# Moving context's residual and norm, half of a modulation, and the deal of fill work in a two-layer hybrid mixer

## The chip, the cores and the metric

The kernel runs on one core of a Trainium2 chip. The metric is the device time of one execution in microseconds, as the median of several runs. A core has five engines that this text names as the profile does: PE (TensorE, matmuls; PEld is its weight load), DVE (VectorE), ACT (ScalarE), POOL (GpSimd) and SP, which here only issues DMAs. Each engine takes its instructions in program order, and an instruction that waits holds up those behind it.

## The reference

Two layers act on 256 latent tokens x and 256 context tokens, 1024 wide, in fp32. Each layer normalises and modulates its input, makes one wide projection from it, feeds three token mixers (rwkv-7, neighbourhood attention, differential attention), merges the three by gates, and projects back. Cut to what matters:

```python
for l in range(2):
    mod_x, mod_c = silu(c) @ w_mod[l] + b_mod[l], silu(c_ctx) @ w_mod[l] + b_mod[l]   # shift, scale, gate
    hx  = rmsnorm(x)  * (1 + sc_x) + sh_x
    hcn = rmsnorm(hc) * (1 + sc_c) + sh_c
    z = h @ w_in[l]                            # inputs of the three mixers, their gates, the merge gates
    o = rwkv7(z), neighbourhood(z), differential(z)
    yb = stack([o_b * silu(g_b)]) @ w_branch[l]              # three branches
    y = sum(sigmoid(mg) * yb) @ w_out[l]
    x  = x  + gt_x * rmsnorm(y_x)
    hc = hc + gt_c * rmsnorm(y_c)              # not in the last layer
return x
```

## The kernel before

Every matmul is done in three passes over fp32r halves (`mm3`): each weight chunk is loaded by SP into a `wr` tile (256 KB, 128x512), ACT copies its high part to `wh`, DVE subtracts to get the low part `wl`, and PE does high by high, high by low and low by high. All operations go through helpers, so the profile's lines are the helpers': L164 ACT, L167 DMA, L179 reduction, L185 two tensors, L189 tensor and scalar, L192 scalar and two tensors, L195 matmul, L199 transpose. A framework places tiles in pools, sets the semaphores and orders each engine's instructions; `keep_in_program_order` pins some of them to the order of the code. General tiles come from one slab of 52 slots, named `k`; PSUM tiles are named `z`, `a`, `b` and `y`.

A layer runs as follows. `rwkv` and `attn` are generators of main work, with waits on chains of small operations, and `weave` deals fill work beside them: after each step of the main generator the table `yl` (L142, one dict for each layer) says how many microseconds of fill are owed, and fill is taken until the debt is paid. The fill is the wide projection's chunks for later mixers (`z_pair`, matmuls of 128x256 or 128x512), gates, merge gates, and the merges of the first two branches. In `yl`, `step` is what is paid after an rwkv step, `qq` and `inv` after parts of the triangular inverse, `diff` after a unit of differential attention and `nd` after the norm of a pair of its heads. A pair of numbers is indexed by segment, head pair or half of the queries; in layer 1 only the first number of `diff` is ever used.

Then `merge(l, 2)` does the third branch: eight output blocks `dt`, each 12 matmuls of 128x512, with wb loads on SP, merge gates `md` loaded on POOL's queue, and POOL adding the blocks. `merged` splits the sums. `outproj` multiplies by wo in 16 chunks and calls `ahead(i)` after each chunk's split, which loads rows of x and context (`rows_load`), loads the next layer's modulation weights wm (`mod_load`, 32 chunks of 256 KB into slab slots), and takes steps of `mod_rows`. A step of `mod_rows` multiplies one wm chunk (`y<-k,cs`); after each eight of them it adds a bias row on DVE (`k<-y,k`, L185), transposes it on PE (`z<-cst,k`) and stores scale and shift for a quarter of the features (`mA`, `mB`). `derived` makes a dozen small per-layer constants on DVE, in a fixed order.

`outproj` ends with `done(t)` for the four token tiles: tiles 0 and 1 are x, and get `residual` (square sum, rsqrt by small DVE operations, two `k<-y,s,k`) and `norm_row` (squares on ACT, rsqrt, scaling) at once; tiles 2 and 3 are context and are put off to `late`. `stream_in` transposes normed rows to features and modulates them. `start_next` starts the next layer with x alone: a `z_pair` for rwkv, the late context rows (`ctx[0]`), the two chunks of the first gate (`gates`: `z_pair`, a tanh on ACT, a multiply `gs<-gs,z` on DVE, a store), and then context's `stream_in` (`ctx[1]`).

Of the kernel before, what the change touches and what calls it, by code (L numbers as in the profile page):

```python
# [134 lines left out]
class K:  # L135
    def __init__(self, tc, io, out):
        self.tc, self.nc, self.io, self.out = tc, tc.nc, io, out
        self.n = 0
        self.have = {}
        self.in_order = False  # L140

        self.yl = [dict(inv=(57, 42.0), qq=(6, 12.07), step=(6, 6), na=(2.5, 1.19), diff=(2.3, 2.9), q=(1.0, 1.0), nd=(2.75, 5), A=(0, 0), B=(0, 4), G=(0.75, 0), C=(5.6, 7.2)),  # L142
                   dict(inv=(23, 51), qq=(3.0, 1.5), step=(6, 6), na=(1.0, 2.3), diff=(4.69, 8.12), q=(1.0, 1.0), nd=(0, 2), A=(0, 0), B=(4.5, 0), G=(0.75, 0), C=(4.0, 6.0))]


    def count(self):
# [335 lines left out]
    def start_next(self, l, P, nr, ctx):  # L482

        r = self.now(self.z_pair(l, 0, 0, nr))
        self.rwkv_rows(l, P, 0, 1, r, 0, nr, False)
        ctx[0]()
        self.now(self.gates(l, nr, 0))
        ctx[1]()
        self.rwkv_wa(l, P, self.now(self.z_pair(l, 6, 0, T)), 0, T)
        row = [self.rwkv_rows(l, P, 0, w, self.now(self.z_pair(l, c, 0, T)), 0, T, True) for w, c in ((0, 2), (2, 4))]  # L490
        self.have["rx", l, 0] = True
        self.have["rz", l, 0] = row[0], [None, None], row[1]
# [889 lines left out]
    def run(self):  # L1382
        tc, nc, io = self.tc, self.nc, self.io
        with ExitStack() as es:
            pool = lambda name, bufs, **kw: es.enter_context(tc.tile_pool(name=name, bufs=bufs, **kw))
            self.const = pool("const", 1)
            self.par = pool("par", 1)
            self.slab = pool("slab", NSLOT)
            self.wr, self.wh, self.wl = pool("wr", 6), pool("wh", 5), pool("wl", 4)
            self.k4 = pool("k4", 7)  # L1390
            self.smp = pool("smp", 8)
            self.pi = pool("pi", 1)
            self.inv = pool("inv", 1)
            self.st = pool("st", 1)
            self.gs, self.gl = pool("gs", 2), pool("gl", 2)
            self.psp = pool("psp", 2, space=PSUM)
            self.psb = {"z": 3, "y": 1}
            dr = pool("dr", 1, space=DRAM)
            dt_ = lambda n, shape: dr.tile(list(shape), F32, tag=n, name=n)
            pairs = lambda n, l, m: [dt_(f"{n}{l}_{i}", (128, 2, T)) for i in range(m)]  # L1400
            self.gd = [pairs("gd", l, 6) for l in range(L)]
            self.md = [pairs("md", l, 12) for l in range(L)]
            self.od = [pairs("od", l, 2) for l in range(L)]
            self.qd = [[pairs(f"qd{w}_", l, 2) for w in range(2)] for l in range(L)]
            self.kd = [[pairs(f"kd{w}_", l, 2) for w in range(2)] for l in range(L)]
            self.rd = [[dt_(f"rd{l}_{g}", (128, 2, 3, T)) for g in range(2)] for l in range(L)]
            self.vd = [[dt_(f"vd{l}_{w}", (128, 4, 512)) for w in range(2)] for l in range(L)]
            self.td = [dt_(f"td{l}", (4, 2, 256)) for l in range(L)]
            self.xd = dr.tile([NX, 1024], F32, tag="xd", name="xd")
            self.cvec()  # L1410
            xs = []
            for t in range(4):
                o = self.k4.tile([128, 2, 512], F32, tag="k4", name=f"x{t}")
                self.dma(self.nc.sync, o, io["xt"][128 * t:128 * t + 128].rearrange("p (a b) -> p a b", a=2))
                xs.append([o[:, 0, :], o[:, 1, :]])
            cst = self.const.tile([128, NCC], F32, tag="cst", name="cst")
            self.dma(nc.gpsimd, cst, io["cst"])
            for k, (a, b) in CCOL.items():
                setattr(self, k, cst[:, a:b])
            P = self.params(0)  # L1420
            ws = []
            self.start(0, P, xs, self.mod_rows(0, P, ws), ws)
            for l in range(L):
                last = l == L - 1
                nq = NX if last else T
                acc = [None] * 8
                PN = None if last else self.params(l + 1)

                def mods():
                    if l == 0:  # L1430
                        yield from self.mod_gate(l, P)
                    if not last:
                        yield from self.mod_gate(l + 1, PN)

                def zs():
                    if l == 0:
                        yield from self.gates(l, nq, 0)
                    if l == 0:
                        yield from self.gates(l, nq, 1)
                        yield from self.rwkv_z(l, P, 1, 0, T, T)  # L1440
                    else:
                        yield from self.rwkv_z(l, P, 1, 0, T, nq)
                        yield from self.gates(l, nq, 1)
                    yield from self.mgates(l, nq, 0)
                    yield from self.attn_z(l, 0, nq)
                    yield from self.attn_z(l, 1, nq)
                    yield from self.gates(l, nq, 2)
                    yield from self.mgates(l, nq, 1)
                    yield from self.mgates(l, nq, 2)

                fill = self.chain(self.both(mods(), zs()), self.merge(l, 0, acc, nq), self.merge(l, 1, acc, nq))
                self.weave(self.rwkv(l, P, last), fill, False)
                self.weave(self.attn(l, P, last), fill)
                self.now(self.merge(l, 2, acc, nq))
                s = self.merged(acc, nq)
                xsrc = io["xt"] if l == 0 else self.xd

                ws, xs, late = [], [], []
                if not last:
                    self.derived(l + 1, PN)  # L1460
                    self.h_new()
                    mod = self.mod_rows(l + 1, PN, ws)

                def ahead(i):
                    if i % 4 == 3 and i // 4 < (2 if last else 4):
                        self.rows_load(xsrc, i // 4, xs)
                    if not last:
                        self.mod_load(l + 1, ws, 2 * i - 4)
                        for _ in range(2 if i > 6 else 0):
                            next(mod)  # L1470

                def rows(t, y, ss):
                    self.residual(t, y, ss, xs[t], last)
                    if not last:
                        self.norm_row(xs[t])

                def done(t, y, ss):
                    if t < 2:
                        rows(t, y, ss)
                    else:  # L1480
                        late.append((t, y, ss))

                self.outproj(l, s, 1 if last else 2, ahead, done)
                if not last:
                    self.mod_load(l + 1, ws, 32)
                    self.now(mod)
                    self.stream_in(PN, xs[0:2], 0)
                    self.start_next(l + 1, PN, NX, (lambda: [rows(*a) for a in late],
                                                    lambda: self.stream_in(PN, xs[2:4], 1)))
                P = PN  # L1490
# [63 lines left out]
```

## Time and profile before

| what | value |
|---|---|
| runs | 1428.95, 1429.24, 1432.83 us, median 1429.24 |
| profiled execution | 1424.81 us, its span 1423.1 us |
| mean granted TensorE clock | 0.966 of full speed |
| PE busy | 1320.4 us (93%) |
| PEld busy | 1098.9 us (77%) |
| DVE busy | 995.7 us (70%) |
| ACT busy | 779.2 us (55%) |
| POOL busy | 233.6 us (16%) |
| moved by DMA | 212.42 MB, mean 149 GB/s |

Times in views are from the start of the span. Layer 0's third merge begins at 737 us, the output projection at 759, and layer 1's first projection matmul stands at 833.13. The idle time that a row of the timeline gives in brackets lies just ahead of that instruction, and the name behind the arrow is what ended it.

### The profile page before, as it was taken

Reading aid. Unit: us, or ns where it says so; the run is one execution under the profiler, and the core shown is the slowest. Engines: PE = TensorE matmul, PEld = TensorE weight load, DVE = VectorE, ACT = ScalarE, POOL = GpSimd, SP = SyncE. Lnnn points to the kernel's source line nnn. Section 1 sums busy time; section 2 is a strip of 40 time slices with the busy share of each in tenths; the row PEclk is TensorE's granted clock in tenths of the full one; section 3 lists DMA queues with packets and bytes.
Section 4 is the critical chain, followed back from the end, with each engine's and each line's share of the span. In section 5 each row is a group of like instructions: output and inputs, shape, how many; then the busy total and the mean of one; then the engine's idle time right before and its main releaser. Section 6 shows DMA issues by size and latency. Waiting matters only on the chain. (4 is left out here: it accounts for less than half of the span.)

```text
span 1423.1 us, 28637 instructions
## 1 busy us (share of the span) xinstructions
PE 1320.4 (93%) x10784; PEld 1098.9 (77%) x10784; DVE 995.7 (70%) x2117; ACT 779.2 (55%) x1734; POOL 233.6 (16%) x292
## 2 busy tenths in 40 slices
PE   6998999999999999998999889998999999999897
PEld 4866777889779876677778777888878789867687
DVE  4763469836898368778685386768848893679886
ACT  5462375336863446667433255866449634467653
POOL 0010011012110012224253000101111000122441
PEclk9999999999999999999999999999889999999899
DMA  9466642424324267432545844354513252685454
GB/s 356 129 196 200 208 130 82 128 68 157 119 80 121 77 185 222 155 105 93 178 145 168 324 127 119 113 177 126 170 56 105 68 148 69 182 272 154 141 166 154
DMA packets 112987, 212.42 MB, mean 149 GB/s; under 512 B 13088, under 2 KB 24880, under 8 KB 112848
## 3 DMA queue, kind: packets, MB, share of 16 engines
q1 hardware_dynamic: 102896, 178.33, 40.6%
q0 software_dynamic: 9952, 32.26, 7.0%
q8 instruction: 85, 1.39, 0.4%
q14 instruction: 54, 0.44, 0.1%
HBM read 176.70 MB, written 33.83 MB: 148 GB/s over the span
## 5 line engine op out<-in xcount | busy, mean ns | idle before, releaser
L195 PE MATMUL z<-k,wh 128*128 128x512 f32 (+1 forms) x2352 | 653.9, 361 | 8.8 <-ACT wh L164 4.2
L195 PEld LDWEIGHTS z<-k,wh 128*128 128x128 f32 x2352 | 417.8, 194 | 76.2 <-issue 9.1
L195 PE MATMUL z<-k,wl 128*128 128x512 f32 (+1 forms) x1176 | 421.7, 360 | 7.3 <-DVE wl L185 7.3
L164 ACT ACTIVATE wh<-wr 128x512 fp32r<-128x512 f32 x376 | 235.4, 630 | 317.8 <-PE z L195 212.7
L185 DVE TENSOR_TENSOR wl<-wr,wh 128x512 fp32r<-128x512 f32 x376 | 278.5, 747 | 157.7 <-PE z L195 59.9
L195 PEld LDWEIGHTS z<-k,wl 128*128 128x128 f32 x1176 | 227.1, 194 | 42.8 <-DVE wl L185 12.1
L195 PE MATMUL z<-wh,k 128*128 128x256 f32 x736 | 145.1, 291 | 2.6 <-ACT k L164 1.3
L195 PEld LDWEIGHTS z<-wh,k 128*128 128x128 f32 x736 | 119.6, 196 | 5.7 <-DVE k L192 2.1
L195 PE MATMUL z<-wl,k 128*128 128x256 f32 x368 | 106.7, 290 | 0.6 <-DVE wl L185 0.6
L185 POOL TENSOR_TENSOR k<-k,k 64x512 fp32r<-64x512 f32 (+3 forms) x64 | 78.0, 1222 | 154.9 <-ACT k L164 62.1
L164 ACT ACTIVATE gs<-z 128x512 f32<-128x512 f32 (+1 forms) x134 | 66.7, 500 | 53.5 <-PE z L195 44.1
L164 ACT ACTIVATE k<-k 64x256 fp32r<-64x256 f32 (+5 forms) x146 | 74.8, 537 | 32.0 <-POOL k L185 20.3
L185 DVE TENSOR_TENSOR k<-k,k 128x256 fp32r<-128x256 f32 (+5 forms) x134 | 76.0, 580 | 12.0 <-ACT k L164 9.3
L199 PE MATMUL b<-cst,k 128*128 128x128 f32 x368 | 65.1, 286 | 17.6 <-DVE k L189 5.6
L164 ACT ACTIVATE k<-a,s 128x512 f32<-128x512 f32 (+1 forms) x96 | 59.2, 617 | 33.1 <-DVE s L179 32.1
L195 PEld LDWEIGHTS z<-wl,k 128*128 128x128 f32 x368 | 72.2, 196 | 1.4 <-DVE wl L185 1.0
L199 PEld LDWEIGHTS b<-cst,k 128*128 128x128 f32 x368 | 42.9, 144 | 37.6 <-issue 15.0
L164 ACT ACTIVATE k<-b 128x256 f32<-128x256 f32 (+1 forms) x144 | 62.8, 465 | 16.5 <-PE b L199 15.8
L195 PE MATMUL a<-k,k 128*128 128x512 f32 (+1 forms) x192 | 61.1, 404 | 10.0 <-ACT k L164 6.1
L195 PE MATMUL a<-ar,bk 64*128 64x128 f32 (+1 forms) x512 | 51.1, 288 | 9.6 <-ACT Lab L164 8.8
L195 PEld LDWEIGHTS a<-ar,bk 64*128 64x128 f32 x512 | 43.5, 190 | 21.3 <-ACT Lab L164 15.7
L179 DVE TENSOR_REDUCE s<-a 128x1 f32<-128x512 f32 (+1 forms) x96 | 56.4, 588 | 1.2 <-PE a L195 1.0
(175 smaller groups left out, 1899.4 us busy)
## 6 DMA issues: line engine op xcount, KB each, us to landing
wr<-in_wi SPq DMA_DIRECT2D x296, 256.0 KB, 3.1
k<-in_wm SPq DMA_DIRECT2D x64, 256.0 KB, 5.4
wr<-in_wb SPq DMA_DIRECT2D x48, 256.0 KB, 2.6
md<-gs SPq DMA_DIRECT2D x36, 256.0 KB, 2.9
k<-md POOLq DMA_DIRECT2D x36, 256.0 KB, 4.5
wr<-in_wg SPq DMA_DIRECT2D x32, 256.0 KB, 3.4
wr<-in_wo SPq DMA_DIRECT2D x32, 256.0 KB, 4.0
gd<-gs SPq DMA_DIRECT2D x18, 256.0 KB, 3.2
```

The lines of the kernel that those rows point to most:

```text
L164: return self.nc.scalar.activation(out=out, in_=in_, func=func, **kw)
L179: return self.nc.vector.tensor_reduce(out=out, in_=in_, axis=AX.X, op=op, **kw)
L185: return (eng or self.nc.vector).tensor_tensor(out=out, in0=a, in1=b, op=op)
L195: return self.nc.tensor.matmul(out, lhsT=lhsT, rhs=rhs, start=start, stop=stop)
L199: return self.nc.tensor.transpose(out, in_, self.ident[0:k, 0:k])
```

## The change

Three edits. In `run`, layer 0 calls `derived` and makes the generator `mod_rows` before the third merge instead of after it, loads 4 wm chunks ahead and then 4 more in each of the merge's steps, and takes four steps of `mod_rows` in each; in `ahead`, one more wm chunk is loaded at each call (instead of two), and one step is taken at calls 2 to 11 (instead of two at calls 7 to 15). In `start_next`, the first chunk of the gate comes ahead of context's residual and norm, the second behind it. In `yl`, layer 1's `qq`, `step`, `diff` and `nd` have other numbers.

```diff
-                   dict(inv=(23, 51), qq=(3.0, 1.5), step=(6, 6), na=(1.0, 2.3), diff=(4.69, 8.12), q=(1.0, 1.0), nd=(0, 2), A=(0, 0), B=(4.5, 0), G=(0.75, 0), C=(4.0, 6.0))]
+                   dict(inv=(23, 51), qq=(0, 1.5), step=(6, 4.5), na=(1.0, 2.3), diff=(5.86, 16.24), q=(1.0, 1.0), nd=(0, 5.0), A=(0, 0), B=(4.5, 0), G=(0.75, 0), C=(4.0, 6.0))]
...
+        self.now(self.gates(l, nr, 0, (0,)))
         ctx[0]()
-        self.now(self.gates(l, nr, 0))
+        self.now(self.gates(l, nr, 0, (1,)))
         ctx[1]()
...
-                self.now(self.merge(l, 2, acc, nq))
+                ws, xs, late = [], [], []
+                if last:
+                    self.now(self.merge(l, 2, acc, nq))
+                else:
+
+                    self.derived(l + 1, PN)
+                    mod = self.mod_rows(l + 1, PN, ws)
+                    self.mod_load(l + 1, ws, 4)
+                    for i, _ in enumerate(self.merge(l, 2, acc, nq)):
+                        self.mod_load(l + 1, ws, 4 * i + 8)
+                        for _ in range(4):
+                            next(mod)
                 s = self.merged(acc, nq)
...
-                        self.mod_load(l + 1, ws, 2 * i - 4)
-                        for _ in range(2 if i > 6 else 0):
+                        self.mod_load(l + 1, ws, 18 + i)
+                        if 2 <= i < 12:
                             next(mod)
```

What this moves is seen in the order of the instructions. The first place is SP's queue around the third merge (wb) and the output projection (wo). Before, wm begins behind the last of a run of wo and two loads of rows:

```order
L167 DMA wr_8918<-in_wo 128x512
L167 DMA wr_8960<-in_wo 128x512
L167 DMA wr_9002<-in_wo 128x512
L167 DMA k_8705<-in_xt 128x512
L167 DMA k_8706<-in_xt 128x512
L167 DMA k_8709<-in_wm 128x512
L167 DMA k_8711<-in_wm 128x512
```

Now it begins ahead of the merge's last wb chunk:

```order
L167 DMA wr_8522<-in_wb 128x512
L167 DMA wr_8589<-in_wb 128x512
L167 DMA k_8343<-in_wm 128x512
L167 DMA k_8345<-in_wm 128x512
L167 DMA k_8347<-in_wm 128x512
L167 DMA k_8349<-in_wm 128x512
L167 DMA wr_8595<-in_wb 128x512
L167 DMA wr_8721<-in_wo 128x512
L167 DMA wr_8751<-in_wo 128x512
L167 DMA wr_8781<-in_wo 128x512
L167 DMA k_8417<-in_wm 128x512
L167 DMA k_8419<-in_wm 128x512
```

Twenty wm loads now stand between the last two wb and the sixth wo; the other twelve come one at a time between the later wo. On PE, 15 of the 32 wm chunks are multiplied among the third merge's matmuls, 9 between the projection's chunks and 8 behind its end (before: none, 16 and 16).

The second place is DVE in the passage to layer 1. `y,s,k` is the residual of the last context tile, `gs_9750` the first gate chunk's multiply, `gs_9830` the second's, and `s` are the small operations of the norms. Before:

```order
L185 TENSOR_TENSOR s_9643<-s_9644,s_9643 128x1
L192 SCALAR_TENSOR_TENSOR k_9187<-y_8606,s_9643,k_9187 128x512
L192 SCALAR_TENSOR_TENSOR k_9188<-y_8606,s_9643,k_9188 128x512
L179 TENSOR_REDUCE s_9660<-s_9655 128x1
L189 TENSOR_SCALAR s_9662<-s_9660 128x1
L192 SCALAR_TENSOR_TENSOR gs_9750<-gs_9750,z_9676 128x256
L189 TENSOR_SCALAR s_9664<-s_9662 128x1
L192 SCALAR_TENSOR_TENSOR gs_9750<-gs_9750,z_9677 128x256
L189 TENSOR_SCALAR s_9665<-s_9664,s_9662 128x1
L192 SCALAR_TENSOR_TENSOR gs_9830<-gs_9830,z_9756 128x256
```

Now `gs_9676` is the first chunk's multiply, and it stands around four splits of weights, ahead of the reduction of the other context tile:

```order
L192 SCALAR_TENSOR_TENSOR gs_9676<-gs_9676,z_9602 128x256
L185 TENSOR_TENSOR wl_9761<-wr_9758,wh_9760 128x512
L185 TENSOR_TENSOR wl_9773<-wr_9770,wh_9772 128x512
L185 TENSOR_TENSOR wl_9791<-wr_9788,wh_9790 128x512
L185 TENSOR_TENSOR wl_9809<-wr_9806,wh_9808 128x512
L192 SCALAR_TENSOR_TENSOR gs_9676<-gs_9676,z_9603 128x256
L179 TENSOR_REDUCE s_9703<-s_9698 128x1
```

The residual of the last tile comes 24 rows later, behind the next chunk's splits (`wl_9945` is the last of them), and the second chunk's multiply follows it:

```order
L185 TENSOR_TENSOR wl_9945<-wr_9942,wh_9944 128x512
L189 TENSOR_SCALAR s_9723<-s_9722,s_9723 128x1
L189 TENSOR_SCALAR s_9724<-s_9723,s_9721 128x1
L189 TENSOR_SCALAR s_9724<-s_9724 128x1
L185 TENSOR_TENSOR s_9723<-s_9724,s_9723 128x1
L192 SCALAR_TENSOR_TENSOR k_9246<-y_8718,s_9723,k_9246 128x512
L192 SCALAR_TENSOR_TENSOR k_9247<-y_8718,s_9723,k_9247 128x512
L179 TENSOR_REDUCE s_9740<-s_9735 128x1
L189 TENSOR_SCALAR s_9742<-s_9740 128x1
L192 SCALAR_TENSOR_TENSOR gs_9830<-gs_9830,z_9756 128x256
```

So the first gate chunk passed context's chain, and context's chain passed the next chunk's weight splits.

The third place is PE at the end of differential attention in layer 1, where `z<-k,wh` and `z<-k,wl` are fill and all else is main work. Before, the last fill row of a longer run without fill, and what follows:

```order
L195 MATMUL z_15720<-k_8582,wl_15802 128x256
L199 MATMUL b_15621<-cst,k_15541 128x128 x4
L195 MATMUL b_15658<-k_15233,cst 128x256
L195 MATMUL b_15664<-k_15236,cst 128x256
L195 MATMUL y_15628<-k_14874,k_15626 128x128
L195 MATMUL y_15628<-k_14875,k_15626 128x128
L195 MATMUL y_15628<-k_14878,k_15626 128x128
L195 MATMUL y_15628<-k_14879,k_15626 128x128
L195 MATMUL a_15751<-k_15443,k_15442 128x512 x2
L195 MATMUL a_15761<-k_15451,k_15450 128x512 x2
L199 MATMUL b_15774<-cst,k_15640 128x128 x4
L195 MATMUL a_15827<-k_15671,k_15670 128x512 x2
```

Now 43 fill rows stand ahead of the place that `a_15827` has in that row, of which the last is shown:

```order
L195 MATMUL z_15750<-k_8694,wl_15802 128x256
L195 MATMUL a_15827<-k_15635,k_15634 128x512 x2
L195 MATMUL a_15837<-k_15643,k_15642 128x512 x2
L199 MATMUL b_15850<-cst,k_15724 128x128 x4
L195 MATMUL y_15857<-k_14778,k_15747 128x128
L195 MATMUL y_15857<-k_14779,k_15747 128x128
L195 MATMUL y_15857<-k_14782,k_15747 128x128
L195 MATMUL y_15857<-k_14783,k_15747 128x128
L195 MATMUL a_15999<-k_15635,k_15634 128x512 x2
L195 MATMUL a_16009<-k_15643,k_15642 128x512 x2
L195 MATMUL y_15857<-k_14778,k_15855 128x128
L195 MATMUL y_15857<-k_14779,k_15855 128x128
```

Before, 24 rows of main work stood together without fill (12 of them shown); now there are 14. The fill for it came out of the rwkv steps of layer 1's second segment, where 138 fill matmuls in three steps (54, 48 and 36) became 108 (24, 54 and 30).

## Rows read from the trace of the kernel before

**Rows 1.** The page, section 1: busy time, share of the span, instructions.

```profile
PE 1320.4 (93%) x10784; PEld 1098.9 (77%) x10784; DVE 995.7 (70%) x2117; ACT 779.2 (55%) x1734; POOL 233.6 (16%) x292
```

**Rows 2.** Timeline of PE: start, duration, operation, count, [idle before <- what ended it].

```profile
768.71 0.39 PE L195 MATMUL z<-wl,k 128*128 128x256 f32 x1 [0.59 <-DVE wl L185]
...
770.50 0.38 PE L195 MATMUL z<-wh,k 128*128 128x256 f32 x1 [1.28 <-ACT k L164]
...
786.22 0.64 PE L195 MATMUL y<-k,cs 128*32 128x128 f32 x16
...
802.33 0.48 PE L199 MATMUL z<-cst,k 128*128 128x128 f32 x1 [5.14 <-DVE k L185]
```

**Rows 3.** Timeline of DVE behind that gap, same columns.

```profile
795.11 0.69 DVE L185 TENSOR_TENSOR wl<-wr,wh 128x512 fp32r<-128x512 f32 x1 [9.23 <-ACT wh L164]
...
801.99 0.28 DVE L185 TENSOR_TENSOR k<-y,k 128x128 f32<-128x128 f32 x1
```

**Rows 4.** Waits of ACT, 773 to 823: us in total, times, longest.

```profile
ACT wh L164 <- DMA wr<-in_wo: 14.8, 5, 9.0
```

**Rows 5.** DMA issues from 773 to 807: count, KB each, median us to landing.

```profile
k<-in_wm SPq DMA_DIRECT2D x32, 256.0 KB, 5.3
```

**Rows 6.** Busy time by stretch: length, engines (instructions), PE clock, DMA share, GB/s.

```profile
730.00:760.00 30.00, 28.72 (x132) 23.41 (x131) 21.53 (x32) 9.70 (x17) 17.79 (x17) 1.00 0.51 158
...
780.00:807.00 27.00, 21.81 (x206) 19.41 (x206) 5.73 (x14) 5.72 (x18) 0.00 (x0) 0.89 1.03 369
800.00:810.00 10.00, 7.67 (x63) 6.60 (x67) 3.66 (x10) 3.87 (x13) 0.00 (x0) 0.66 1.03 364
822.84:833.13 10.29, 7.57 (x141) 5.83 (x141) 8.61 (x40) 5.37 (x17) 1.08 (x2) 0.76 0.47 153
...
1187.80:1200.31 12.51, 12.51 (x216) 11.84 (x215) 4.87 (x6) 5.96 (x11) 1.54 (x1) 1.00 0.27 66
1326.87:1342.96 16.09, 11.57 (x56) 8.52 (x56) 13.01 (x30) 11.04 (x29) 7.84 (x10) 0.79 0.43 135
```

**Rows 7.** Timeline of PE in the passage to layer 1.

```profile
848.25 0.40 PE L195 MATMUL z<-k,wh 128*128 128x256 f32 x2
848.49 0.28 PE L195 MATMUL z<-k,wl 128*128 128x256 f32 x1
...
854.35 0.51 PE L195 MATMUL z<-k,wh 128*128 128x256 f32 x2 [2.61 <-DVE gs L192]
...
860.63 0.33 PE L199 MATMUL a<-cst,k 128*128 128x128 f32 x1 [1.66 <-ACT k L164]
```

**Rows 8.** Timeline of DVE in the same passage.

```profile
827.67 0.16 DVE L179 TENSOR_REDUCE s<-s 128x1 f32<-128x2 f32 x1
...
830.95 0.48 DVE L189 TENSOR_SCALAR k<-k,s 128x512 f32<-128x512 f32 x1
...
851.39 1.42 DVE L192 SCALAR_TENSOR_TENSOR k<-y,s,k 128x512 f32<-128x512 f32 x2
853.60 0.15 DVE L179 TENSOR_REDUCE s<-s 128x1 f32<-128x2 f32 x1 [0.80 <-ACT gs L164]
...
853.87 0.42 DVE L192 SCALAR_TENSOR_TENSOR gs<-gs,z 128x256 f32<-128x256 f32 x1
...
860.07 0.48 DVE L189 TENSOR_SCALAR k<-k,s 128x512 f32<-128x512 f32 x1
```

**Rows 9.** Timeline of PE at the end of layer 1's differential attention.

```profile
1328.18 0.70 PE L195 MATMUL b<-k,cst 128*128 128x256 f32 x2 [0.25 <-ACT k L164]
...
1330.93 0.73 PE L195 MATMUL a<-k,k 128*128 128x512 f32 x2 [0.69 <-ACT k L164]
1332.58 0.66 PE L199 MATMUL b<-cst,k 128*128 128x128 f32 x4 [0.92 <-DVE k L192]
1335.52 1.22 PE L195 MATMUL a<-k,k 128*128 128x512 f32 x2 [2.28 <-ACT k L164]
```

**Rows 10.** Timeline of SP's DMA queue: the last three wb loads.

```profile
729.72 4.45 SPq L167 DMA_DIRECT2D wr<-in_wb  x3
```

More of the change, by code (lines that the diff above doesn't have):

```diff
@@ L1453, in run @@
                 self.weave(self.attn(l, P, last), fill)
-                self.now(self.merge(l, 2, acc, nq))
+                ws, xs, late = [], [], []
[9 more added lines that the diff above has]
+                            next(mod)
                 s = self.merged(acc, nq)
                 xsrc = io["xt"] if l == 0 else self.xd
-                ws, xs, late = [], [], []
                 if not last:
-                    self.derived(l + 1, PN)
                     self.h_new()
-                    mod = self.mod_rows(l + 1, PN, ws)
                 def ahead(i):
```

## The prediction

> **What bounds the kernel now.** I read the page's busy times first: TensorE works 1320.4 of 1423.1 us [rows 1]. With so little idle time, a change that only moves work can gain in two ways: by closing a gap of TensorE, or by keeping its clock at the upper of its two levels, 2.4 GHz, where it otherwise stands at 1.2. So the next views are the timeline of TensorE around the three places that the edit touches (what ended each idle time stands in brackets), and then, for each gap, the engine that is named there, until something is found that is not itself waiting.
>
> *Place one: layer 0's third merge and output projection.* The longest gap is at 802.33: 5.14 us before a small transpose that turns a row of the modulation [rows 2]. Its releaser is a row addition on VectorE at 801.99, behind weight splits, of which one had waited 9.23 us for ScalarE's copy [rows 3], and those copies waited 14.8 us, in five waits, for loads of wo [rows 4]. The loads were late because all 32 chunks of wm, 256 KB each, were asked for here [rows 5], and in 780 to 807 the queues moved 369 GB/s at a DMA share of 1.03 [rows 6]: the DMA engines were full. Just ahead, in 730 to 760, they moved 158 GB/s [rows 6]. After the gap the mean granted clock of 800 to 810 was 0.66 [rows 6]. A second trouble is at the projection's start: waits of 0.59 and 1.28 us between 768 and 771, the second for the chain that adds and splits the merged sums [rows 2].
>
> *Place two: context's residual and norm in the passage to layer 1.* TensorE waits 2.61 us at 854.35 for a gate's multiply on VectorE, and 1.66 us at 860.63 for context's normed rows [rows 7]. The multiply stood at 853.87, behind the fourth token tile's two residual instructions at 851.39 and a reduction at 853.60 [rows 8].
>
> *Place three: the end of layer 1's differential attention.* No fill is left there: 1326.87 to 1342.96 has TensorE busy for 11.57 of 16.09 us at a clock of 0.79 [rows 6], with waits of 0.25, 0.69, 0.92 and 2.28 us in its first half [rows 9]. In the rwkv steps fill is plentiful: from 1187.80 to 1200.31 TensorE has no idle time at all [rows 6].
>
> **The change part by part.** No instruction is added or removed; each part is a matter of place.
>
> *wm and modulation beside the third merge.* All the 5.14 us should go: the loads of wo no longer stand in the crowd, and 15 of the 32 chunks' matmuls are done before the projection starts. With the gap goes the low clock: 10 us at 0.66 lose 3.4 us of full speed, of which some 0.9 fall in idle time; I take 2.5. The 1.9 us at 768 to 771 I take whole, because the modulation's matmuls of 15 chunks, some 5 us at the price below, now lie among the merge's blocks and give the chain of its sums that much time. Against it, work comes ahead of the projection's end: the modulation's small matmuls, 16 in the records for two chunks, take 0.64 us inside the projection [rows 2], so 8 chunks take 2.6; 24 chunks instead of 16 now lie ahead of the projection's end, so plus 2.6. Behind the end 8 chunks remain, but there the norm chain of x binds and not TensorE: 7.57 us busy of 10.29 [rows 6], so taking work out gives nothing there. Sum: -5.1 - 2.5 - 1.9 + 2.6 = **-6.9 us**. Bounds: -10, if the modulation's matmuls fill idle time in the merge; -2, if loads hold back the merge.
>
> What hides the moved loads is the merge itself. In the new order 20 chunks of wm stand on SP's queue from just ahead of the last wb chunk to behind the fifth wo. The last three wb were issued around 730 [rows 10]. 158 GB/s for 30 us are 4.7 MB; 20 chunks of 256 KB add 5.2 MB; 9.9 MB in 30 us are 332 GB/s, under the 369 that were seen, with 10% to spare. The last wb, which four wm loads are now ahead of, was issued some 20 us ahead of its use near the merge's end at 759, so a delay of a few microseconds is hidden.
> The Trainium skill (page "Trainium Kernel Development and Optimization", section Key Constraints) says that transfers from the SP, ACT and POOL queues run on the same 16 DMA engines and interleave. It speaks against this part: the merge's md loads on POOL's queue are no refuge from the wm loads on SP's. The trace bears it out in so far as the wo loads were late in the crowd, and the sum with it would be the first rival's, below. The page "DMA: Bandwidth & Descriptors" (section Specifications) gives about 358 GB/s as HBM's limit for a core; the trace has 369 over 27 us, and by the page the 9.9 MB would take 27.7 instead of 26.8 of the 30 us, which changes nothing.
>
> *derived's small operations* move to the merge's start, on VectorE: a dozen short ones; at 0.15 us each, as the reduction in [rows 8], some 2 us where VectorE runs 21.53 of 30 us [rows 6]. Taken as 0, bounds 0 to +2 (a split that comes later, then a wait of TensorE).
>
> *Context between two gate chunks.* The gates' first chunk comes ahead of context's chain, so the multiply no longer stands behind the residual and the 2.61 us wait goes. But the chain itself starts later. Count from 848.25, the start of the second gate chunk's 48 matmuls, which now run without a break: at 0.12 us each, by the rows' starts, 5.8 us. The last weight split of the next chunk waits for them (0.69 by [rows 3], and about as much for the copy ahead of it: 7.1), then some 0.9 us of small operations and the fourth tile's residual to its reduction, 2.2 us as from 851.39 to 853.60: 10.2. From reduction to norm 3.3 us where little stands between (827.67 to 830.95) and 6.5 where splits that wait stand between (853.60 to 860.07) [rows 8]; in the new order two gate multiplies of 0.4 us stand between and no split, so 4.1: 14.3. Then 0.5 to the transposes: 14.8. Before it was 860.63 - 848.25 = 12.4 [rows 7]. So this part costs **+2.4 us**: one idle time of some 8 us where there were 2.6 and 1.7. Bounds: -0.5 (the split does not wait) to +5.6 (the reduction to norm takes 6.5 us and the clock is low behind it).
>
> *The new deal of layer 1.* Only numbers that reach layer 1 count: qq 3 to 0, the second step 6 to 4.5, diff 4.69 to 5.86, nd's second 2 to 5. The order shows 43 fill matmuls now standing where the stretch without fill began, and the bare stretch of 24 rows cut to 14. The four waits in [rows 9], 4.1 us, come ahead of or inside those 43 matmuls (5.2 us at 0.12), and the clock of 0.79 over 16 us loses 3.4 us; with the waits gone perhaps half of that. That is up to -5.8. The fill comes out of the rwkv steps, where nothing was idle: a step falls from 54 to 24 fills, 12.51 to some 8.9 us, and may then wait on its own chain. No row shows a step with so little fill; a lower bound is nothing, an upper the 3.6 us that were taken. I take +1.5 in all for the steps and for neighbourhood attention, which starts earlier against its own loads, and of the gain 4.5: **-3 us**, bounds -5.8 to +2.
>
> **Sum.** -6.9 + 2.4 - 3 = -7.5 us on the profiled execution's 1424.81 us, so 1417.3. That execution was 4.4 us under the median of the three runs shown, 1429.24; on the median it gives **1421.7 us**.
>
> **The rivals.** A difference under 0.3% (4.3 us) can't be told from none here.
> (a) *The merge is not a free cover*: md and wo loads are late by a few microseconds as wm crowds 730 to 760 (10% of the rate is all that is spare). Half of the first gain is given back: 1429.24 - 3.5 + 2.4 - 3 = 1425.1. For it: POOL's loads share the engines. Against: the rate stays under what was seen. Chance 0.15, two thirds of it within 0.3%.
> (b) *The new deal gives nothing*, or context's chain takes its upper bound: -6.9 + 2.4 + 1 or -6.9 + 5.6 - 3, so 1425 to 1426. For it: steps with 24 fills were never seen. Chance 0.20, two thirds of it within 0.3%.
> (c) *Slower*: the rate beside the merge. If, with small packets and three queues at once, the DMA engines move only 230 GB/s in place of 332, then 9.9 MB take 43 us, the merge and projection stall for 13 us, and -7.5 turns into +5.5: 1434.7. It decides from 237 GB/s down, where the stall is 11.8 us. Against it: 369 GB/s with the same kinds of chunk. For it: loads, stores and two queues are mixed here, and the mean was 158. Chance 0.13.
> (d) *More*: the modulation fills idle time and layer 1's end has its clock back: -10 + 1 for context - 5.8, so 1414.4. Chance 0.07.
> The forecast itself, 1418.5 to 1424.5, has 0.45.
>
> **Numbers.** Faster by over 0.3%: 0.45 + 0.07 + a third of (a) and (b), 0.64. Within 0.3%: the rest of (a) and (b), 0.23. Slower: (c), 0.13. The range reaches from inside (d) to just short of (c), 1414 to 1432.5, and leaves out 0.13 above and some 0.04 below.
>
> **What would show it.** TensorE has no gap over 1 us from 737 to the projection's end, which comes 6 to 8 us earlier; wm's loads fall between 730 and 755 at over 300 GB/s, and wo's waits on ScalarE fall under 4 us. In the passage one gap of 7 to 10 us stands before context's transposes in place of 2.61 and 1.66. In layer 1 the 2.28 us gap is gone, and the rwkv steps are 9 to 10 us long without gaps over 1 us. It would be wrong if TensorE waits for a wl split or for md inside the merge, if the passage's gap is over 12 us, or if the rwkv steps show gaps.

## The result, and the profile after

The changed kernel takes 1410.4 us (median of four runs, 1406.25 to 1412.29) against 1429.1 (four runs, 1426.55 to 1432.83): a ratio of 0.9863, 95% interval 0.9832 to 0.9894. On the chip of the first four experiments it was 1412.1 against 1427.9 us, ratio 0.9901 (0.9876 to 0.9925). It is 14 to 20 us faster by the two ratios (15.8 and 18.7 by the medians) where 7.5 were forecast, and 1410.4 lies below the range that began at 1414.0.

The profiled execution has a span of 1404.6 us. Its stretches, each from a landmark on TensorE to the next, are the third merge with the output projection (the merge alone in the second row), the projection's end to layer 1's first projection matmul, from there to the first that acts on x and context together, and layer 1 from its first rwkv score matmul to the end. The rows behind that cut layer 1: first inverse to second; second inverse to neighbourhood attention's first values; of that, one rwkv step of 8.7 us; on to the first values of differential attention; and to the end. The columns are those of [rows 6].

```profile
735.17:814.95 79.78, 78.63 (x676) 68.66 (x674) 46.28 (x103) 28.47 (x71) 22.57 (x24) 1.00 0.70 242
735.20:763.70 28.50, 27.35 (x219) 20.52 (x217) 21.68 (x41) 9.76 (x20) 16.97 (x17) 1.00 0.86 305
814.95:824.46 9.51, 4.34 (x77) 3.27 (x76) 8.59 (x39) 5.65 (x19) 1.08 (x2) 0.91 0.50 166
824.46:857.42 32.96, 25.03 (x168) 22.93 (x167) 25.18 (x74) 18.42 (x41) 1.46 (x2) 0.81 0.44 132
...
907.38:1404.56 497.18, 457.14 (x4362) 407.14 (x4361) 386.16 (x793) 297.87 (x671) 89.02 (x111) 0.96 0.47 145
1016.15:1159.64 143.49, 136.76 (x1389) 119.08 (x1390) 109.39 (x225) 89.68 (x194) 15.36 (x20) 0.94 0.34 100
1159.64:1237.40 77.76, 72.33 (x1166) 66.07 (x1166) 46.26 (x80) 35.80 (x70) 10.56 (x11) 0.93 0.47 138
1175.10:1183.80 8.70, 8.70 (x184) 8.03 (x181) 3.49 (x4) 3.60 (x6) 1.54 (x1) 1.00 0.07 24
1237.40:1291.60 54.20, 52.14 (x351) 41.29 (x351) 47.96 (x106) 42.51 (x111) 15.04 (x17) 1.00 0.69 218
1291.60:1404.56 112.96, 95.67 (x725) 89.55 (x723) 90.70 (x205) 60.21 (x143) 34.52 (x41) 0.96 0.52 164
```

The same stretches before, without those of [rows 6]:

```profile
737.03:822.84 85.81, 78.53 (x615) 69.84 (x617) 41.79 (x100) 26.96 (x69) 23.04 (x25) 0.96 0.70 237
833.13:861.94 28.81, 23.32 (x163) 21.75 (x161) 23.13 (x70) 17.20 (x38) 0.72 (x1) 0.91 0.45 133
...
912.82:1423.11 510.29, 464.88 (x4362) 411.37 (x4361) 387.56 (x793) 298.41 (x671) 88.42 (x111) 0.95 0.47 141
1021.84:1173.00 151.16, 142.11 (x1401) 123.06 (x1402) 110.63 (x226) 90.06 (x194) 16.48 (x21) 0.92 0.33 97
1173.00:1257.20 84.20, 78.82 (x1214) 72.41 (x1214) 48.92 (x84) 40.38 (x80) 10.66 (x11) 0.95 0.49 141
1257.20:1314.30 57.10, 54.38 (x356) 41.82 (x356) 49.45 (x106) 42.34 (x110) 15.04 (x17) 0.99 0.67 208
1314.30:1423.10 108.80, 89.28 (x660) 82.88 (x658) 86.63 (x199) 56.10 (x135) 33.25 (x41) 0.93 0.50 155
```

The merge with the projection fell from 85.8 to 79.8 us: the merge itself grew from 22 to 28.5, and the projection lost more than that. The passage grew, 28.8 to 33.0. Layer 1 fell from 510.3 to 497.2 with the same 4362 matmul records: 5.4 us less idle time (length less PE busy, 45.4 and 40.0) and 7.7 us less busy time for the same work, at a clock of 0.95 and 0.96. Of the 18.5 us between the two spans, 1.9 lie ahead of the third merge, in code that no edit touches. TensorE's gaps after, on its timeline, against [rows 2], [rows 7] and [rows 9]:

```profile
740.24 0.50 PE L195 MATMUL z<-k,wh 128*128 128x512 f32 x1 [0.75 <-DVE k L185]
...
819.24 0.30 PE L199 MATMUL z<-cst,k 128*128 128x128 f32 x1 [1.71 <-DVE k L185]
...
822.99 0.48 PE L199 MATMUL a<-cst,k 128*128 128x128 f32 x1 [3.45 <-ACT k L164]
...
854.58 0.48 PE L199 MATMUL a<-cst,k 128*128 128x128 f32 x1 [6.52 <-ACT k L164]
...
1322.69 0.73 PE L195 MATMUL a<-k,k 128*128 128x512 f32 x2 [0.86 <-ACT k L164]
...
1327.56 0.41 PE L199 MATMUL b<-cst,k 128*128 128x128 f32 x2 [1.58 <-DVE k L185]
```

The 5.14 us ahead of the transpose and the 1.28 at the projection's start are gone, and nothing over 1 us stands between the merge's start and the projection's end. Behind the end 1.71 us stand before the modulation's last transpose, for its row addition on VectorE (1.8 before), and 3.45 before x's normed rows (0.5 before). In the passage one gap of 6.52 us took the place of 2.61 and 1.66. At the end of differential attention 0.86, and one of 0.34 at 1319.68, are left of the four waits; the 1.58 at 1327.56 was 1.41 before, at the same place. ScalarE's waits for wo, against [rows 4]:

```profile
ACT wh L164 <- DMA wr<-in_wo: 3.0, 1, 3.0
```

### The profile page after: what moved, and what is told of

Its sections match the earlier page's. It is cut to its first block, busy times and chain, and to the rows that moved or that the text cites. A ratio compares the mean times of both kernels' runs of the same rounds, so it can differ in the third digit from the quotient of the medians.

```text
span 1404.6 us, 28623 instructions
## 1 busy us (share of the span) xinstructions
PE 1309.1 (93%) x10784; PEld 1091.4 (78%) x10784; DVE 998.9 (71%) x2117; ACT 779.5 (55%) x1734; POOL 234.1 (17%) x292
## 4 chain that ended last, share of the span: by engine, by line
PE 37%; DVE 14%; ACT 6%; issue 3%; DMA 1%; SPq 0%; POOL 0%; DVEq 0%; ACTq 0%; POOLq 0%
PE z L195 22%; PE a L195 8%; ACT k L164 3%; PE y L195 3%; DVE wl L185 3%; DVE k L185 3%; PE b L199 2%; PE b L195 2%; DVE X L182 1%; DVE k L192 1%; DVE s L179 1%; DVE s L189 1%; ACT wh L164 1%; ACT gs L164 1%; DVE tmp L185 1%
## 5 line engine op out<-in xcount | busy, mean ns | idle before, releaser
L199 PE MATMUL b<-cst,k 128*128 128x128 f32 x368 | 65.7, 286 | 18.5 <-DVE k L189 7.1
L199 PEld LDWEIGHTS b<-cst,k 128*128 128x128 f32 x368 | 42.3, 143 | 39.4 <-issue 14.8
L195 PEld LDWEIGHTS a<-ar,bk 64*128 64x128 f32 x512 | 42.1, 187 | 20.4 <-ACT Lab L164 14.8
```

The costliest lines, as they stand in the source:

```text
L195: return self.nc.tensor.matmul(out, lhsT=lhsT, rhs=rhs, start=start, stop=stop)
L199: return self.nc.tensor.transpose(out, in_, self.ident[0:k, 0:k])
```

## The experiments

All ratios are to the kernel before, on the same chip as the run. The time up to layer 0's third merge scatters, so a stretch of the profile tells small effects better than the whole. Layer 1 is the stretch that begins at 907.38 in the rows of after; with the old deal it took 510.3, 512.8, 513.6 and 510.1 us (before and three kernels below), mean 511.7. With the whole new deal it took 497.5, 497.2, 499.9 and 497.1, mean 497.9. So a single profile places a kernel's layer 1 to some 2 us either way.

| run | what is changed of before | ratio, 95% interval | merge and projection | passage | layer 1 |
|---|---|---|---|---|---|
| before | nothing | 1 | 85.8 | 28.8 | 510.3 |
| e1_deal | the whole deal | 0.9896 (0.9870 to 0.9922) | 85.6 | 27.4 | 497.5 |
| e2_context | context's place | 1.0027 (1.0009 to 1.0046) | 85.5 | 32.0 | 512.8 |
| e3_mod | wm and modulation | 0.9988 (0.9965 to 1.0011) | 79.6 | 30.0 | 513.6 |
| e4_after | all three | 0.9901 (0.9876 to 0.9925) | 79.6 | 31.8 | 499.9 |
| e5_qq | qq | 0.9969 (0.9944 to 0.9995) | 83.8 | 28.9 | 508.5 |
| e6_tail | step, diff, nd | 0.9931 (0.9904 to 0.9958) | 85.9 | 28.8 | 507.6 |
| e7_no_context | deal, wm and modulation | 0.9848 (0.9827 to 0.9869) | 79.6 | 29.1 | 497.1 |
| e8_no_deal | context, wm and modulation | 0.9978 (0.9957 to 0.9999) | 79.6 | 32.5 | 510.1 |
| e9_qq_step | qq, step | 0.9927 (0.9895 to 0.9958) | 84.7 | 28.9 | 502.2 |
| e10_qq_diff | qq, diff, nd | 0.9945 (0.9922 to 0.9967) | 85.4 | 27.8 | 505.3 |
| e11_diff | diff, nd | 1.0046 (1.0025 to 1.0066) | 83.8 | 28.9 | 518.4 |
| e12_more | as e7_no_context, step 3.5 | 0.9853 (0.9823 to 0.9883) | 79.6 | 29.1 | 495.2 |
| e13_step | step | 0.9940 (0.9915 to 0.9964) | 85.1 | 28.9 | 507.6 |
| e14_spare | spare matmuls, old deal | 1.0014 (1.0000 to 1.0028) | 85.6 | 28.9 | 512.1 |

**The three parts, each alone.** `e1_deal` has only the changed line of `yl`, `e2_context` only the changed lines of `start_next`, `e3_mod` only those of `run`, all as in the diff above; `e4_after` is the whole.

> The kernel before with the changed numbers of layer 1's deal alone. Theory D (the term that was mis-sized is the deal: its idle time and its low-clock periods in layer 1 went from the rwkv steps of the first segment to the end of differential attention): 9 to 13 us faster than before. Theory P (the prediction's three terms are right, and what lies beyond them is the scatter of runs): 3 us faster. Theory C (the parts act together: the passage's new timing sets where low-clock periods fall in layer 1): 3 to 6 us faster alone, and the three parts alone don't add up to the whole.

> The kernel before with context's chain between the two gate chunks alone. Prediction's term: 2.4 us slower, with one gap of about 8 us before context's transposes. Rival from the trace after (one gap of 6.5 us there): 1 to 2 us slower or no change. Theory C: could be faster, if it has less low clock behind it.

> The kernel before with wm's loads and half the modulation beside the third merge alone. Prediction's term: 6.9 us faster, the 5.14 us gap gone, wo's loads no longer waited for. Theory C: less than 5 or more than 9 us, by where the norm chain behind the projection ends.

> The changed kernel again, on the chip on which the three parts run. Theory D: 16 to 20 us faster, and the three parts add up to that within 3 us. Theory P: some 8 to 12 us faster, the earlier runs having been lucky ones. Theory C: 16 to 20 us, with the parts adding up to less than 13.

The deal alone took 1410.9 us against 1427.9, about 15 us by its ratio: nearest to theory D, though above its 9 to 13. The whole took 14 on the same chip, under the 16 that theory D began at. Context's place costs 0.27%, 3.9 us, and 3.2 in its stretch of the profile, where the one gap is 6.52 us as in the changed kernel. The modulation's part is within the noise as a ratio, but its stretch takes 79.6 to 79.8 us in the six kernels that have it and 83.8 to 85.9 in the ten that don't, 5.5 less in the mean. The parts add up (-15 - 2 + 4 against -14, within their intervals), so the coupling that theory C wanted isn't needed.

The kernels below give two more pairs for each part, by their ratios. The modulation: `e8_no_deal` is 7.0 us faster than `e2_context`, and `e7_no_context` 6.9 faster than `e1_deal`. Context's place: `e4_after` is 7.6 us slower than `e7_no_context`, but `e8_no_deal` 1.4 faster than `e3_mod`. With intervals of 3 to 5 us for such a difference, the modulation gains and context's place costs, and the sizes are better taken from the stretches.

**The deal in two.**

```diff
- qq=(3.0, 1.5), step=(6, 6),   diff=(4.69, 8.12),  nd=(0, 2)
+ qq=(0, 1.5),   step=(6, 6),   diff=(4.69, 8.12),  nd=(0, 2)      e5_qq
+ qq=(3.0, 1.5), step=(6, 4.5), diff=(5.86, 16.24), nd=(0, 5.0)    e6_tail
```

> Of the deal, only layer 1's qq of the first segment, 3 to 0 (fill is paid later, in the steps and the second segment). Theory Q (half of the deal's gain lies between the first and the second inverse of layer 1, where the profile of the deal alone has 2.3 us less idle time and 3.4 us less lost to the low clock): 4 to 7 us faster. Theory T (the gain lies at the end of differential attention, and the earlier part only puts fill off): 0 to 1 us faster.

> Of the deal, only step, diff and nd (fill goes from the second segment's rwkv steps to the end of differential attention). Theory Q: 7 to 10 us faster, the rest being with qq. Theory T: 12 to 15 us faster, as the whole deal. The prediction's working has 3 us for this part.

By the ratios, 4.4 and 9.9 us; by the stretch of layer 1, 3.2 and 4.1 where the whole deal has 13.8 (mean of the four profiles with the whole deal and step 4.5, 497.9). By the ratios both lie where theory Q has them, and together they make the whole (14.3 against 15); by the stretch they make 7.3 of 13.8. Theory T isn't excluded by the ratios alone, since the intervals of qq and tail reach 3 to 4 us to either side; against it speaks the stretch, where the tail gains 4.1 and not the whole. Whether the two alone fall short of the whole is not settled. What one profile of each shows is where each may give something back. For qq alone, layer 1's four stretches, cut as above:

```profile
1027.00:1171.10 144.10, 137.43 (x1389) 119.98 (x1390) 109.48 (x225) 89.47 (x194) 15.36 (x20) 0.94 0.33 100
1171.10:1257.90 86.80, 81.42 (x1238) 75.93 (x1238) 51.10 (x86) 40.46 (x81) 10.48 (x11) 0.92 0.49 145
1257.90:1313.20 55.30, 52.09 (x352) 41.42 (x352) 48.99 (x107) 42.34 (x111) 15.46 (x17) 1.00 0.69 214
1313.20:1425.29 112.09, 91.17 (x652) 83.93 (x651) 87.62 (x198) 56.51 (x134) 32.77 (x40) 0.91 0.46 148
```

Between the inverses it has the whole gain of the changed kernel: 144.1 us, as 143.5 after, against 151.2 before, with 12 matmul records fewer (1.4 us of fill at 0.12). At the end it loses: 112.1 us against 108.8 before, with 8 records fewer. The fill that was held back has gone into the rwkv steps (1238 records from the second inverse on, 1214 before), and none of it reaches the end.

**The parts crossed with the passage.**

> The changed kernel with context's chain back ahead of both gate chunks: the modulation beside the merge and the deal stay. If the parts add up (deal -15, merge -2 to -6, context +4): 17 to 21 us faster than before, so 3 to 4 us faster than the changed kernel. If the placing of context's chain only pays together with the others: no faster than the changed kernel.

> The changed kernel with the old deal: the two edits of the passage together. If they add up: 2 us faster to 2 us slower than before (merge -2 to -6, context +4). The prediction's terms: 4.5 us faster.

The edits are `e4_after` with context's lines, or the deal's line, put back. Without context's new place the kernel takes 1407.7 us against 1428.4, ratio 0.9848, and its interval lies just below that of `e4_after`. So the best of these kernels leaves that edit out. `e8_no_deal` comes out 3 us faster than before, by its ratio, between the two forecasts.

**Which of the deal's numbers.** Three more combinations, and one that goes further:

```diff
+ qq=(0, 1.5),   step=(6, 4.5), diff=(4.69, 8.12),  nd=(0, 2)      e9_qq_step
+ qq=(0, 1.5),   step=(6, 6),   diff=(5.86, 16.24), nd=(0, 5.0)    e10_qq_diff
+ qq=(3.0, 1.5), step=(6, 6),   diff=(5.86, 16.24), nd=(0, 5.0)    e11_diff
+ qq=(0, 1.5),   step=(6, 3.5), diff=(5.86, 16.24), nd=(0, 5.0)    e12_more
```

> Of the deal, qq 3 to 0 and the second step 6 to 4.5, with the old diff and nd. Theory B (what counts is how much fill is still in hand at the end of differential attention, and qq and step alone decide that): 10 to 14 us faster than before, with no stretch without fill at the end of differential attention. Theory R (the fill that was saved must also be dealt out by diff and nd, or it is left over behind the attention): 4 to 7 us faster, as the sum of the small parts.

> Of the deal, qq 3 to 0 with the new diff and nd, but the old step of 6. Theory B: 3 to 5 us faster, as qq alone, since the rwkv steps still take the fill; the stretch without fill (22 rows) stays near 16 us. Theory R: 8 to 12 us faster.

> Of the deal, only diff and nd; qq and step as before. Theory B: 0 to 2 us faster; less fill is in hand by then, and only where it stands changes. Theory R: 6 to 9 us faster, the most of the tail's part.

> The changed kernel with context's chain back ahead of both gate chunks, and layer 1's second step at 3.5 instead of 4.5, so that still more fill is left for the end. Theory B: 0 to 3 us faster than with 4.5, if the rwkv steps, now with less fill than any that was run, show no waits; where they do, up to 4 us slower than with 4.5. In all 17 to 24 us faster than before.

qq with step gains 10 us by its ratio and 9.5 by its stretch: nearer to theory B than to R. qq with diff and nd gains 8 and 6.4, between the two. Neither theory had what diff and nd do alone: 0.46% slower. TensorE's timeline there:

```profile
1340.21 1.04 PE L195 MATMUL z<-k,wh 128*128 128x256 f32 x3 [5.06 <-ACT k L164]
...
1382.35 1.09 PE L199 MATMUL b<-cst,k 128*128 128x128 f32 x4 [3.94 <-DVE k L185]
```

The same fill is spent sooner, and then waits of 5.06 and 3.94 us stand where none so long stood before. The first stands ahead of the fill itself: ScalarE's copy for it waits 3.18 us on its own timeline for a load (`k<-od`), so this fill was asked for before its input was there, and the main work behind it waited too. So diff and nd don't make anything by themselves; with qq changed they add some 3 to 4 us (`e10_qq_diff` to `e5_qq`, the whole deal to `e9_qq_step`), and with step alone changed nothing clear (`e6_tail` to `e13_step`: 0.0 by the stretch, 1.3 by the ratio). With step 3.5 the stretch is another 2 us shorter and the ratio the same within its interval; the step with the least fill still shows no wait.

**Two open questions:** whether step pays alone, and whether the low clock or the waits make a stretch without fill dear.

```diff
+ qq=(3.0, 1.5), step=(6, 4.5), diff=(4.69, 8.12),  nd=(0, 2)      e13_step
...
             s = self.ps("a", (128, 128 * nk))
+            if last and (qt, h) in ((1, 2), (0, 3), (1, 3)):
+                for _ in range(3):
+                    self.mm(s, self.h[0][0][:, 0:128], self.h[0][0], True, True)
             sc[h][m](s, slice(128 * qt, 128 * qt + 128), k0)
```

> Of the deal, only the second step, 6 to 4.5; it completes the eight combinations of qq, step and diff with nd. Theory A (fill that is held back pays by itself, each source adding the same): 5 to 7 us faster, as step brought beside qq. Theory I (the parts need each other): step alone 0 to 2 us faster, because the old qq has spent the fill in the first segment before it could be held back.

> The kernel before with 18 spare matmuls of 128x512 at the end of layer 1's differential attention, three ahead of each of the last six score tiles, written into the tile that the scores then overwrite. They do no useful work; the old deal stays. They stand where TensorE waits and where its clock is low. Theory K (the low clock is the larger part of what the stretch without fill costs): its clock rises, and the stretch gets 1 to 3 us shorter although work was added. Theory W (the waits are the cost, and the low clock only stretches work that a chain of DVE and ACT would have delayed anyway): the stretch gets no shorter, or up to 4 us longer by the spare work that isn't hidden.

step alone gains 4.1 us by the stretch and 8.6 by its ratio, so it pays alone, as theory A has it, though its size isn't settled.

With these the eight combinations are complete, and layer 1 as a whole splits into two effects. Three of them, layer 1 from the same landmark to the end, in the order `e13_step`, `e10_qq_diff`, `e9_qq_step`:

```profile
915.33:1422.93 507.60, 466.19 (x4362) 414.95 (x4361) 385.88 (x793) 299.14 (x671) 89.26 (x111) 0.94 0.47 142
```

```profile
911.34:1416.63 505.29, 459.25 (x4362) 410.23 (x4361) 387.03 (x793) 298.10 (x671) 88.32 (x111) 0.95 0.46 143
```

```profile
908.52:1410.70 502.18, 462.31 (x4362) 413.38 (x4361) 384.20 (x793) 297.17 (x671) 90.49 (x111) 0.94 0.47 144
```

`e14_spare` with its added work aside, idle time (length less PE busy) is 37 to 43 us in every kernel with step at 4.5 or 3.5, and 45 to 51 in every kernel with step at 6. Busy time for the same 4362 matmul records, which a low clock stretches, is 457.0 to 460.6 us where qq and diff with nd are both changed, and 462.3 to 467.8 elsewhere. So step takes out idle time, qq together with diff and nd takes out busy time at the low clock, and the whole deal has both.

With the spare matmuls (`e14_spare`) the stretch of differential attention from its first values to its last, before and with them:

```profile
1314.30:1365.50 51.20, 43.88 (x296) 38.87 (x295) 41.74 (x98) 32.21 (x79) 14.71 (x19) 0.90 0.47 144
```

```profile
1318.70:1368.80 50.10, 44.51 (x313) 39.32 (x313) 41.94 (x99) 32.17 (x79) 14.79 (x19) 1.00 0.48 147
```

And its timeline, where `a<-k` are the spare matmuls:

```profile
1333.99 0.95 PE L195 MATMUL a<-k 128*128 128x512 f32 x3
...
1339.99 0.96 PE L195 MATMUL a<-k 128*128 128x512 f32 x3 [2.28 <-ACT k L164]
```

The clock rose from 0.90 to 1.00 over the stretch, which is 5.1 us of full speed, and the 18 spare matmuls take 4.7 us by the rows' starts. The whole stretch is 1.1 us shorter, at the low end of theory K. But cut at the first row of fill, into the part without fill and the fill behind it, before and with the spare matmuls:

```profile
1326.87:1343.47 16.60, 11.84 (x57) 8.55 (x57) 13.45 (x33) 11.55 (x31) 8.07 (x11) 0.79 0.44 140
1343.47:1357.83 14.36, 12.79 (x88) 12.17 (x89) 10.44 (x31) 6.36 (x14) 2.65 (x4) 0.88 0.55 160
```

```profile
1331.33:1348.90 17.57, 13.86 (x75) 10.52 (x75) 14.29 (x37) 11.47 (x31) 9.23 (x12) 1.00 0.44 137
1348.90:1361.18 12.28, 11.41 (x89) 10.69 (x89) 9.81 (x26) 6.38 (x14) 1.53 (x3) 1.00 0.59 182
```

The part without fill, which the two theories are about, is 1.0 us longer, as theory W has it, and the wait of 2.28 us is still there. What was gained, 2.1 us, lies in the fill behind it. So the run doesn't decide between the two theories. Layer 1 as a whole takes 512.1 us, as with the old deal, and the kernel isn't faster (ratio 1.0014). Keeping the clock up with work that nobody needs gave nothing in the end.

## Why the prediction was wrong

**Right: the merge and projection.** -6.9 us were worked out, -6.0 measured between the two profiles and -5.5 in the means of six and ten. The gap of 5.14 went, wo's waits fell from 14.8 to 3.0 us, and the clock of the stretch is 1.00 where it was 0.96. The merge itself grew by 6.5 us: the 15 modulation chunks take 4.0 by their rows' starts, where some 5 were allowed; 1.1 are new waits for splits on VectorE, 0.75 of them at 740.24, where `derived`'s small operations now stand just ahead of the split (they were taken as 0, with bounds of 0 to +2); the other 1.4 stand in no wait. The rival of a merge that is no free cover didn't come: the merge ran at 305 GB/s, under the 369 of [rows 6], and no wait of TensorE in it goes back to a load. The Trainium skill (page "Trainium Kernel Development and Optimization", section Key Constraints) spoke against the part by its rule on queues that share the 16 DMA engines; the trace shows later landings beside the wm loads (from 728 to 758 a median of 6.1 us for md against 5.0 before, and 7.4 for wo against 4.1), and no price in TensorE's time. The crowd that had made wo late before was almost all on SP's own queue, so it did not bear on that rule. That the norm chain of x binds behind the end was right too: with half the modulation's matmuls gone, the stretch only fell from 10.3 to 9.5 us, with TensorE busy for 4.34 of them, and four kernels with the old modulation took 9.5 as well.

**Right in its chain, and near in size partly by luck: context's chain.** +2.4 us were forecast, +3.0 to +4.2 measured against the kernel before (31.8, 32.0, 32.5 and 33.0 in the four profiles that have it, against 28.8; the other profiles without it took 27.4 to 30.0). The one gap that was forecast at 8 us is 6.5, with 0.5 ahead of it. The steps stand in the order that was worked out, on VectorE's timeline, against [rows 8]:

```profile
843.37 0.15 DVE L179 TENSOR_REDUCE s<-s 128x1 f32<-128x2 f32 x1 [0.95 <-ACT gs L164]
...
847.56 0.69 DVE L185 TENSOR_TENSOR wl<-wr,wh 128x512 fp32r<-128x512 f32 x1
...
849.09 1.41 DVE L192 SCALAR_TENSOR_TENSOR k<-y,s,k 128x512 f32<-128x512 f32 x2
851.31 0.15 DVE L179 TENSOR_REDUCE s<-s 128x1 f32<-128x2 f32 x1 [0.80 <-ACT gs L164]
...
853.80 0.49 DVE L189 TENSOR_SCALAR k<-k,s 128x512 f32<-128x512 f32 x1
```

The first context tile's reduction comes only at 843.37, the last split at 847.56, the residual at 849.09, its reduction 2.2 us later, and the norm 2.5 us after that (4.1 was taken). So from the second gate chunk's start, 840.98 in the changed kernel, to context's transposes it is 13.6 us, where 14.8 were worked out and 12.4 stood before: the counted path loses 1.2, and not 2.4. More than that comes from where the sum had no term. From the transposes to the stretch's end it takes 2.8 us against 1.3, since twelve of them stand there in place of six, at a clock of 0.61 from 848.00 to 857.42; the forecast had a low clock there in its upper bound alone. And 1.4 us lie ahead of the second gate chunk, where the clock is lower too (0.89 from 824.46 to 848.00, against 0.94 from 833.13 to 848.25 before). That the trade loses time, since a wait of 2.6 us is replaced by a longer one, was seen before the run, and `e2_context` and `e7_no_context` show it.

**Wrong: "the new deal of layer 1", sized at -3 us.** It measured -13.8 in the stretch and about -15 by the ratio. Two steps of that term failed.

First, no term at all was worked out for qq. Its change was named, and the working then went only to the end of differential attention. The stretch between layer 1's two inverses fell from 151.2 to 143.5 us. Of this, 12 fewer fill matmuls are 1.4 us; the rest, some 6 us, is idle time (9.1 to 6.7 us) and time at the low clock (0.92 to 0.94). `e5_qq` shows that qq alone does it. The prediction has no row of that stretch and so no term for it: its rows are from the longest gaps, and this stretch has several of 0.5 to 1.8 us.

Second, fill that is moved was charged for leaving the rwkv steps: "+1.5" was taken, and the text held that the steps "may then wait". They don't. The first step with 24 fills takes 8.70 us, without idle time and at full clock; the forecast had 8.9 and the sum should have stopped there. At the end, 65 more matmul records, 7.8 us at 0.12, fit into a stretch that grew by 4.2 us, so the end gained 3.6 net, near the 4.5 that was taken. In neighbourhood attention 2.3 us net were gained (57.1 to 54.2 with 5 records fewer), where the same +1.5 had stood for a loss.

Stretch by stretch, net of the fill that was moved: -6.2 between the inverses, -0.7 to neighbourhood attention, -2.3 in it, -3.6 at the end, together -12.8 in this profile. The experiments show how the numbers belong together. In the profile of `e5_qq` part of qq's gain is given back in the rwkv steps and at the end, where none of its fill arrives; diff and nd lose 6.7 us in layer 1 when no fill was held back (`e11_diff`) and gain some 4 on top of qq and step. Step takes the idle time out, with or without the others. What is shown is which numbers do it and where the time goes; the sizes of the single numbers are known to some 2 to 4 us only. Which of the small waits between the inverses let the clock fall, and why the order that qq gives avoids them, stays open; no run took one of them away by itself.

The rival that had the deal giving nothing, and the one that went slower, are both out; the one that ended below the forecast ("more", at 1414.4) had the right sign with -5.8 for the deal, which was also too little.

## What to carry to other kernels

A table that deals out fill has a budget: what a number takes in one place is missing in another, so every changed number needs its own row, and the sum is made over the whole stretch that shares the fill, with its idle time and its clock, and not at the longest gap. Here, fill taken from steps that had no idle time cost nothing, down to 24 matmuls in a step; giving it out faster at the end lost time when none had been held back, and gained on top of that. And an edit that removes a named wait by delaying another chain should be priced by that chain's end and by what stands behind it: here it cost some 3 us, hidden in a change that gained several times as much.

## What the runs showed that was not expected

The clock was at half in stretches without idle time. From 1160.70 to 1167.50 in the changed kernel TensorE is busy for all 6.80 us, in 155 matmul records, and the granted clock is 0.50; what ran ahead of it and in it were matmuls of 32x32 tiles of the inverse, with a dozen fill matmuls between them. A wait of 1.27 us ends just ahead, at 1159.64. But in the kernel before, at the same inverse, TensorE is busy at a clock of 1.00 for the whole 10 us from 1173.00 (the wait of 1.87 us ahead of them didn't lower it), and the clock falls at the end of a run of 32x32 matmuls with no idle time near. The changed kernel first, then the kernel before:

```profile
1160.70:1167.50 6.80, 6.80 (x155) 6.51 (x151) 4.70 (x6) 2.35 (x4) 0.00 (x0) 0.50 0.28 98
```

```profile
1173.00:1183.00 10.00, 10.00 (x274) 9.78 (x276) 5.89 (x7) 4.16 (x7) 0.00 (x0) 1.00 0.30 95
1183.10:1186.50 3.40, 3.40 (x25) 3.32 (x20) 0.00 (x0) 1.18 (x2) 0.00 (x0) 0.51 0.02 5
```

So in these rows busy time alone didn't keep the upper level. Whether the small matmuls are the cause wasn't tested.

And code that no edit touched scatters: the kernels, in which no edit moves anything ahead of the third merge's last loads, reach the merge between 733.9 and 745.0 us. The first 735 us of two of them, `e9_qq_step` and `e3_mod`:

```profile
0.00:735.00 735.00, 693.29 (x5290) 548.24 (x5291) 502.40 (x1050) 399.63 (x874) 114.90 (x145) 0.99 0.47 149
```

```profile
0.00:735.00 735.00, 693.23 (x5243) 547.27 (x5244) 491.59 (x1035) 395.49 (x866) 108.08 (x139) 0.97 0.47 147
```

TensorE is busy for the same 693 us in both, but in one it got 47 records further, at a clock of 0.99 against 0.97; 0.02 over 735 us are up to 15 us of full speed. A difference of a few microseconds between two profiles is read from the stretch that was changed and not from the span.
